# A float32 tanh-gated double matmul: the stores from the third triple on issued by ScalarE instead of SyncE

## The chip, the cores and the metric

The kernel runs on one core of a Trainium2 chip. A time is the device time of one execution in microseconds. Beside it there is one profiled execution, whose span (first to last instruction of the program) is a little shorter than its device time.

## The reference

```python
def reference(x, w1, w2):          # x (16, 512, 1024), w1 and w2 (1024, 768), all float32
    y1 = np.matmul(x, w1)
    y2 = np.matmul(x, w2)
    return (np.tanh(y1) * y2).astype(np.float32)
```

The 16 x 512 rows of `x` make 64 row tiles of 128. Each gives one output tile of 128 x 768 float32, 384 KB.

## The kernel before

**Arithmetic.** Inputs are cast to float16. The first four row tiles (`HEAD`) are multiplied plainly, eight matmuls for each block of columns. The other 60 go in 20 triples: the 3 row tiles of a triple, the two halves of the inner dimension and three blocks of 512 weight columns are combined by a scheme of the Strassen kind (`C_OPS`): 15 products of four matmuls each in place of 18. Its sums of x operands (`x_sum`, line 425) and of weights are made by VectorE, its sums of results (`c_add`, line 467) by VectorE and its signed copies between banks and SBUF (`c_copy`, line 461) by ScalarE. ScalarE also makes the tanh (`c_tanh`, line 470), VectorE multiplies it by the second result (`c_mul`, line 475), both into an output tile `o`. ScalarE further sums absolute values of every x tile and weight block (line 394), for a flag that would send odd inputs to a general path; it is not taken here.

**The data's way.** GpSimd loads a row tile from HBM with a cast (`load_x`, line 366) into one of 8 buffers `xh`; SyncE transposes it by DMA (`transpose`, line 391) into one of 12 buffers `xT`; GpSimd does not issue load `mt` before the transpose of tile `mt - 4` has landed (`hold_loads`, line 494). Output tiles lie in 9 buffers and go to HBM by `store` (line 431), one DMA for a tile; only those of the last triple and of one early tile go in parts.

**The order.** All instructions are written in an order made by `Planner`, a list scheduler in the kernel's Python. Each operation (`op`) gets its engines with a modelled cost, a due time, what it needs, and what it is to stand behind (`behind`, which sets the order alone). `PE_ORDER` fixes the order of the products. The program then issues each engine's instructions in that order. An engine's queue is in order: an instruction that waits holds up all behind it. The program's framework adds the waits: a store waits for the multiplies into its tile, a tanh for the landing of the store that had the same output buffer. It also gives the DMAs of SyncE and ScalarE eight semaphores in turn, and a DMA waits until the one that had its semaphore before, eight DMAs earlier in the program, has landed. DMAs of GpSimd have eight of their own.

**What the change touches.** Line 731 plans the store of every tile that is neither in the head nor in the last triple. There `i` is the triple, `late` a product of the next triple (`p0`, `p4` or `p12`) behind which the store is to stand. Lines 721, 723 and 729 plan the other stores, the split ones for SyncE or ScalarE as the planner finds room.

Of the kernel before, what the change touches and what calls it, by code (L numbers as in the profile page):

```python
# [74 lines left out]
class Planner:  # L75
# [9 lines left out]
    def op(self, name, engines, due, needs, fn, *args, behind=(), issued=(), chains=(), xfer=0.0, latency=None, seeds=False,  # L85
           lands=None, hold=0.0):
        assert name not in self.ops, name
        self.ops[name] = dict(engines=engines, due=due, needs=[n for n in needs if n], behind=[n for n in behind if n], issued=[n for n in issued if n], fn=fn, args=args,
                              chains=chains, xfer=xfer, latency=latency, seeds=seeds, lands=lands, hold=hold)
        for c in chains:  # L90
            self.chains.setdefault(c, {"left": 0, "bank": None, "end": 0.0, "act": 0.0, "dve": 0.0})["left"] += 1
# [154 lines left out]
def kernel(  # L246
# [66 lines left out]
    def xh_place(mt):  # L313
        return (mt - HEAD) % XH_BUFS
# [7 lines left out]
    op = plan.op  # L322
# [193 lines left out]
    slot_of = {(i, p): ORIGIN + z * SLOT for z, i, p in sequence}  # L516
# [4 lines left out]
    late = [f"b{k}" for s, k in slices if s == "b"]  # L521
# [8 lines left out]
    for n, what in enumerate(on_sp):  # L530
# [3 lines left out]
        else:  # L534
# [4 lines left out]
               behind=[f"c{a}{b}" for a, b in old], lands=lands[what])  # L539
# [3 lines left out]
    for n, mt in enumerate(rows_in):  # L543
        op(f"L{mt}", {"pool": 0.58}, 1 + 0.1 * n, [], load_x, mt, issued=[f"L{rows_in[n - 1]}" if n else f"c{late[-1]}"],
           behind=[f"cx{m}{h}" for m in range(2, HEAD) for h in range(2) if xh_place(m) == xh_place(mt)], lands=lands[f"x{mt}"])
# [8 lines left out]
    for t in range(2):  # L554
        for k in range(KO):
            late = START + 32 + 8 * (t * KO + k)
# [34 lines left out]
    outs = {mt: [] for mt in range(MT)}  # L591

    def reuse_out(mt):
        return [f"st{mt - O_BUFS}"] if mt >= HEAD + O_BUFS else []
# [16 lines left out]
    for n, s in enumerate("agb"):  # L611
        for mt in range(HEAD):
            if (s, mt) == ("b", HEAD - 1):
                continue
            due, behind = (lambda n: landed[slices["agb".index(s) * KO + n]] + 0.8 + 0.02 * mt), [FILL[mt]] if s == "b" and mt in FILL else []
            finals(mt, s, due(KO - 1) + (5.0, 3.0, 7.0)["agb".index(s)], plain(mt, s, due, behind))

    mt = HEAD - 1
# [57 lines left out]
    for i in range(TRIPLES):  # L676
# [3 lines left out]
        for v, a, b, how in A_SUMS:  # L680
            op(f"S{v}.{i}", {"dve": 0.335}, None, x_needs(i, a) + x_needs(i, b), x_sum, i, v, a, b, how,
               hold=needed(i, v) - S_AHEAD if i > 1 else 0.0,
               behind=[f"{r}.{i - S_BUFS}" for r in a_readers[v]] if i >= S_BUFS else first_done)
# [3 lines left out]
        for o in C_OPS:  # L687
# [19 lines left out]
            mt = HEAD + 3 * i + r  # L707
            due = soonest[i, name] + LAST
            if kind in ("t", "th"):
                lo, n = (0, F) if kind == "t" else (F, G)  # L710
                op(f"{name}.{i}", {"act": 0.5 if n == F else 0.285}, due, needs, c_tanh, i, r, o[4], lo, n, o[5],
                   behind=reuse_out(mt) + ([f"{FIRST_READER[name]}.{i}"] if i == TRIPLES - 1 and name in FIRST_READER else []), chains=chains)
# [4 lines left out]
    for mt in range(MT):  # L717
        i = (mt - HEAD) // 3 if mt >= HEAD else -1
        if mt < HEAD:
            kept = mt == HEAD - 1  # L720
            op(f"st{mt}", {"sp": 0.05}, 1e3, outs[mt][:1] if kept else outs[mt], store, mt, F if kept else 0, G if kept else N, behind=[f"p12.{4 + mt}"], xfer=1.0)
            for t in range(2 if kept else 0):
                op(f"st{mt}{chr(88 + t)}", {"sp": 0.4, "act": 0.4}, 2e4, outs[mt][1 + t:2 + t], store, mt, t * G, G, xfer=0.4)
            continue
        late = [f"{('p0', 'p4', 'p12')[(mt - HEAD) % 3]}.{i + 1}"] if i < TRIPLES - 2 else []
        if i == TRIPLES - 1:
            for a, lo, n in ((0, 0, F), (1, F, G)):
                part = outs[mt][a:a + 1]
                op(f"st{mt}{a}", {"sp": 0.4, "act": 0.4}, 2e4, part, store, mt, lo, n, xfer=0.4)
        else:  # L730
            op(f"st{mt}", {"sp": 0.05}, slot_of[max(i, 0), "p2"] + 12, outs[mt], store, mt, behind=late, xfer=1.0)
    for mt in range(BY_PE, MT):
        back = xh_before(mt)
        free = [] if back is None else ([f"PT{back}0", f"PT{back}1"] if back < BY_PE else [f"T{back}"]) + ([f"D{back}"] if back >= HEAD else [])
# [1 line left out]
        if mt >= BY_PE + FREE:  # L736
# [4 lines left out]
           behind=xt_readers[mt - XT_BUFS] if mt >= XT_BUFS and mt - XT_BUFS != HEAD - 1 else [], xfer=1.2, latency=1.0 if mt < HEAD + 6 else 3.0)  # L741
    for mt in range(HEAD, MT):
        i, r = divmod(mt - HEAD, 3)
# [126 lines left out]
```

## Time and profile before

| | us |
|---|---|
| median of 3 runs | 300.72 |
| lowest, highest run | 299.75, 303.65 |
| the profiled execution's own time | 299.0 |
| its span | 297.2 |

The profile names engines PE (TensorE; PEld its weight loads), DVE (VectorE), ACT (ScalarE), POOL (GpSimd) and SP (SyncE). A "q" behind a name (SPq, ACTq) is the engine's instruction queue: issuing a DMA or waiting for a semaphore is work of the queue and is not counted as busy. A DMA's issue has a duration of its own, and its landing (the moment its semaphore is complete) comes later. "A <- B: t, n, m" in the waits view says that A sat idle t us in n waits, the longest m, and that B ended them. In the table by stretch each row gives the stretch's length and then the busy time of each engine with the number of its instructions, the clock that TensorE was granted, the mean busy share of the DMA engines and the rate in GB/s. Matmul durations overlap, since matmuls are pipelined; the distance between their starts is the better measure.

The DMA part of the page:

| issue | queue | count | KB each | median us from issue to landing |
|---|---|---|---|---|
| stores | SP | 60 | 384 | 5.4 |
| loads of x with a cast | POOL | 60 | 256 | 6.7 |
| transposes | SP | 57 | - | 6.6 |
| last stores in parts | SP, ACT | 9 | 128 or 256 | 2.0 to 2.8 |

### The profile page before, as it was taken

To read this page: it belongs to the slowest core of one execution; us is meant where nothing else is said; L and a number is where in the kernel's file an instruction comes from. 1 tells how busy PE (TensorE), PEld (TensorE's weight loads), DVE (VectorE), ACT (ScalarE), POOL (GpSimd) and SP (SyncE) were. 2 spreads that over 40 slices of the span, in tenths; PEclk is the share of its full clock that TensorE was granted. 3 is DMA by queue.
4 is the path that set the end of the run, shared out by engine and by line. 5 is a ranking of instruction groups with operands and counts; after the bars stand their busy time and mean duration, and the time that the engine had idled before them with its cause. 6 is when DMAs were issued, how large, how long until landed. Compare 5 with 4: busy or idle time off the path is not lost. (4 is left out here: it accounts for less than half of the span.)

```text
span 297.2 us, 4671 instructions
## 1 busy us (share of the span) xinstructions
PE 289.5 (97%) x1385; PEld 133.4 (45%) x1385; DVE 254.9 (86%) x539; ACT 226.1 (76%) x454; POOL 51.7 (17%) x129
## 2 busy tenths in 40 slices
PE   7999999999999999999999999999999999999993
PEld 5444444444444444444444444444444444444442
DVE  1669999989999998979989899889889898988884
ACT  3577899699878879797797988768686776868451
POOL 0064036030112210303122121122020200000000
PEclk9999999999999999999999999999999999999999
DMA  6999999999999999999999999999999999741234
GB/s 230 387 298 198 173 158 216 192 166 197 193 238 217 252 228 270 270 171 306 183 220 199 226 292 218 283 278 251 165 279 113 271 85 270 229 161 52 108 140 164
DMA packets 84427, 63.51 MB, mean 214 GB/s; under 512 B 62768, under 2 KB 66608, under 8 KB 84400
## 3 DMA queue, kind: packets, MB, share of 16 engines
q1 hardware_dynamic: 73456, 44.71, 64.0%
q0 software_dynamic: 9792, 16.78, 38.0%
q10 hardware_dynamic: 1152, 1.70, 1.6%
q8 instruction: 11, 0.18, 0.3%
q14 instruction: 16, 0.13, 0.1%
HBM read 39.85 MB, written 25.17 MB: 219 GB/s over the span
## 5 line engine op out<-in xcount | busy, mean ns | idle before, releaser
L457 PE MATMUL bank<-b,early_x 128*128 128x512 f16 x640 | 148.3, 379 | 0.1
L457 PEld LDWEIGHTS <-early_x 128*128 128x128 f16 x800 | 78.2, 98 | 95.1 <-issue 0.7
L461 ACT ACTIVATE arena<-bank 128x512 f32<-128x512 f32 x100 | 59.1, 596 | 33.4 <-PE bank L457 33.3
L467 DVE TENSOR_TENSOR bank<-bank,arena 128x512 f32<-128x512 f32 x100 | 69.6, 696 | 15.5 <-ACT arena L461 7.3
L475 DVE TENSOR_TENSOR o<-o,bank 128x256 f32<-128x256 f32 (+1 forms) x120 | 63.2, 547 | 5.8 <-ACT o L470 5.5
L394 ACT ACTIVATE junk<-xh 128x1024 f16<-128x1024 f16 x60 | 63.3, 1055 | 0.1
L457 PEld LDWEIGHTS <-xT 128*128 128x128 f16 x400 | 39.0, 98 | 46.4
L457 PE MATMUL bank<-b,xT 128*128 128x512 f16 x240 | 58.3, 379 | 0.0
L494 POOL CAST held<-xT 128x1 f32<-128x1 f16 x54 | 15.1, 280 | 163.7 <-DMA xT<-xh 163.7
L470 ACT ACTIVATE o<-bank 128x256 f32<-128x256 f32 (+1 forms) x80 | 34.4, 437 | 12.0 <-DVE bank L467 7.1
L457 PE MATMUL bank<-wh,xT 128*128 128x512 f16 x160 | 41.1, 379 | 0.0
L457 PE MATMUL bank<-wh,early_x 128*128 128x512 f16 x160 | 40.9, 379 | 0.0
L366 POOL DMA_DIRECT2D xh<-in_x_dram x60 | 31.7, 528 | 16.0 <-issue 5.4
L425 DVE TENSOR_TENSOR early_x<-early_x,xT 128x512 f16<-128x512 f16 x80 | 33.5, 418 | 0.6
L461 ACT ACTIVATE bank<-bank 128x512 f32<-128x512 f32 x40 | 21.5, 575 | 7.2 <-DVE bank L467 6.6
L470 ACT ACTIVATE o<-arena 128x512 f32<-128x512 f32 x40 | 25.1, 627 | 1.0 <-DVE arena L467 1.0
L434 PE MATMUL bank<-wh,xT 128*128 128x512 f16 x72 | 18.4, 379 | 1.1 <-DVE wh L372 0.5
L425 DVE TENSOR_TENSOR early_x<-xT,early_x 128x512 f16<-128x512 f16 x40 | 16.7, 418 | 0.0
L425 DVE TENSOR_TENSOR early_x<-xT,xT 128x512 f16<-128x512 f16 x40 | 16.7, 417 | 0.0
L467 DVE TENSOR_TENSOR bank<-arena,bank 128x512 f32<-128x512 f32 x20 | 13.9, 695 | 3.2 <-ACT o L470 1.7
L467 DVE TENSOR_TENSOR arena<-bank,arena 128x512 f32<-128x512 f32 x20 | 13.7, 685 | 1.4 <-ACT arena L461 1.3
L467 DVE TENSOR_TENSOR arena<-arena,bank 128x512 f32<-128x512 f32 x20 | 13.6, 678 | 0.0
(49 smaller groups left out, 135.4 us busy)
## 6 DMA issues: line engine op xcount, KB each, us to landing
out_dram<-o SPq DMA_DIRECT2D x60, 384.0 KB, 5.4
xh<-in_x_dram POOLq DMA_DIRECT2D x60, 256.0 KB, 6.7
arena<-in_w_dram SPq DMA_DIRECT2D x12, 256.0 KB, 5.5
early_x<-in_x_dram SPq DMA_DIRECT2D x8, 256.0 KB, 5.0
arena<-in_w_dram ACTq DMA_DIRECT2D x4, 256.0 KB, 5.9
wh<-in_w_dram POOLq DMA_DIRECT2D x8, 128.0 KB, 5.7
xT<-xh SPq DMA_TRANSPOSE x57, 6.6
out_dram<-o SPq DMA_DIRECT2D x2, 256.0 KB, 2.8
```

The lines of the kernel that those rows point to most:

```text
L366: pin(nc.gpsimd.dma_start(xh(mt), xf[mt]))
L394: pin(nc.scalar.activation(junk[:, :src.shape[-1]], src, ACT.Abs, scale=scale, accum_out=sums[:, column:column + 1]))
L425: pin(engine[e].tensor_tensor(x_operand(i, v), x_operand(i, a), x_operand(i, b), OP[how]))
L434: pin(nc.tensor.matmul(bank(chain)[:, :rhs.shape[-1]], xt(mt)[:, k, :], rhs, start=first, stop=k == KO - 1, skip_group_check=True))
L457: pin(nc.tensor.matmul(place(i, dst), x_operand(i, a)[:, k, :], w_rhs(b, k), start=begins and k == 0, stop=k == KH - 1, skip_group_check=T ...
L461: pin(nc.scalar.activation(place(i, dst), place(i, src), ACT.Copy, scale=float(sign)))
L467: pin(nc.vector.tensor_tensor(place(i, dst), a, b, ALU.add if signs == (1, 1) else ALU.subtract))
L470: pin(nc.scalar.activation(out_tile(HEAD + 3 * i + r)[:, lo:lo + n], place(i, src)[:, :n], ACT.Tanh, scale=float(sign)))
L475: pin(nc.vector.tensor_tensor(o, o, place(i, src)[:, at:at + n], ALU.mult))
L494: pin(nc.gpsimd.tensor_copy(held, xt(mt)[:, 0, :1]))
```

## The change

One line of the plan: for triples 2 to 18 the store's engine is ScalarE, with a modelled cost of 0.35 us, instead of SyncE with 0.05.

```diff
         else:
-            op(f"st{mt}", {"sp": 0.05}, slot_of[max(i, 0), "p2"] + 12, outs[mt], store, mt, behind=late, xfer=1.0)
+            op(f"st{mt}", {"act": 0.35} if i >= 2 else {"sp": 0.05}, slot_of[max(i, 0), "p2"] + 12, outs[mt], store, mt, behind=late, xfer=1.0)
```

In the list of instructions, 51 stores leave SyncE's queue (147 instructions to 96) and stand in ScalarE's (389 to 440), each between two activations. The planner works with the new costs, so from the third triple on some neighbouring instructions of ScalarE and VectorE change places and products use other banks; the order of the products on TensorE stays. Which DMA is the eighth before another changes with the order too.

## The prediction

> **What bounds the kernel now.** I read the page first, its busy times and slices.
>
> ```profile
> span 297.2 us, 4671 instructions
> ...
> PE 289.5 (97%) x1385; PEld 133.4 (45%) x1385; DVE 254.9 (86%) x539; ACT 226.1 (76%) x454; POOL 51.7 (17%) x129
> ...
> PE   7999999999999999999999999999999999999993
> ...
> PEclk9999999999999999999999999999999999999999
> ```
>
> A busy TensorE alone proves little, so I looked at the starts of its matmuls one by one: 216 ns apart without a hole from 35.6 us to the last at 292.5 us, but for one gap of 0.1 us at 285.1. The waits view of PE for 36 to 292 us is empty. All the idle time of TensorE lies in the start (before 36 us, where nothing is edited: the first moved store stands near 74 us) and in the last 4.6 us. So no engine that works faster between 36 and 292 us can shorten the run. The change can only keep this row of matmuls closed or tear it.
>
> The table by stretch says how much room ScalarE has (its column is the fourth after the length).
>
> ```profile
> core 0: us, PE busy (x) PEld busy (x) DVE busy (x) ACT busy (x) POOL busy (x), PEclk, DMA share, GB/s
> ...
> 74.00:125.00 51.00, 51.00 (x238) 23.15 (x237) 46.47 (x98) 42.02 (x88) 9.69 (x26) 1.00 1.16 233
> 125.00:176.00 51.00, 51.00 (x238) 23.12 (x237) 44.75 (x94) 42.91 (x89) 9.76 (x24) 1.00 1.23 227
> 176.00:228.00 52.00, 52.00 (x243) 23.59 (x241) 46.29 (x97) 39.42 (x79) 9.40 (x26) 1.00 1.18 237
> 228.00:280.00 52.00, 52.00 (x244) 23.59 (x242) 46.60 (x101) 37.94 (x76) 2.85 (x8) 1.00 0.78 170
> ```
>
> A triple lasts 60 matmuls, 12.95 us. ScalarE is idle 9.0 of 51 us from 74 to 125 us, so 2.3 us in a triple, and 3.5 us in a triple at the end. It is the waits view that tells what this idleness is.
>
> ```profile
> ACT arena L461 <- PE bank L457: 28.8, 38, 2.9
> ACT bank L461 <- DVE bank L467: 5.5, 10, 0.6
> ```
>
> That is ScalarE of 74 to 280 us: it waits for matmuls (28.8 us), it is ahead. But not far: I followed, from the starts and ends in the timeline, how late each of its instructions could begin before a matmul would start late. The median is 1.0 us, the smallest outside the last triple 0.3 us. Example: the tanh of 102.77 us, then its multiply on VectorE 103.25 to 103.66, then the matmul into that bank at 103.99. A stall of ScalarE over one or two microseconds is a stall of TensorE.
>
> **The change part by part.** Removed: 51 issues from SyncE's queue (triples 2 to 18, three each). Added: the same 51, 384 KB each, on ScalarE's queue, in the instruction listing 3 between some 22 activations of a triple. The bytes are the same. Prices:
>
> ```profile
> L431 SPq DMA_DIRECT2D out_dram<-o x49: 362/529/1112, 75.0 to 255.5; - x49
> ...
> L391 SPq DMA_TRANSPOSE xT<-xh x45: 1232/2080/4261, 71.2 to 253.1; - x45
> ```
>
> These two are SyncE from 74 to 256 us (ns, least/median/most). *Issue on ScalarE:* its own final stores, smaller, took 338 to 363 ns, its loads at the start 406 to 460; the same 384 KB on SyncE 529. I take 0.53, the equal transfer; bounds 0.34 and 1.11. 3 x 0.53 = 1.6 us a triple against 2.3 us idle. It is no activation time, though: the records show ScalarE's queue taking its next instruction when the one before starts to run (a semaphore wait and an activation both at 96.42 us), so 0.53 us lies beside the 0.38 to 1.06 us of the activation ahead. Cost 0; with that cover gone, the idle 0.1 to 1.3 us before the next one and its slack still hide it.
>
> *Wait for the tile:* the planner puts a store behind a matmul of the following triple, so the multiplies it needs ended 0.7 to 7 us before (all but the last triples). Cost 0. In the last triple but one a store waits for its multiply (ended 277.5 us) ahead of a copy that ran at 277.74 with 0.25 us to spare: 277.5 + 0.34 to 0.53 is 0.15 us late to 0.04 us past the slack. Cost 0.
>
> *Wait for a semaphore:* this is what I think decides. In the listing the DMAs of SyncE and ScalarE share eight semaphores in turn, so each waits until the eighth before it has landed. On SyncE that held up nobody but transposes; on ScalarE it holds up the activations behind the store, then VectorE's multiplies, then TensorE's banks. I compared, by the times of before, when the eighth-last landed with when ScalarE gets there. Before 90 us it had landed 0.4 to 2 us earlier, after 180 us 2 to 27 us earlier, but from 94 to 175 us it lands up to 4.5 us later for 16 of 19 stores. The worst:
>
> ```profile
> 95.88 1.55 SPq L431 DMA_DIRECT2D out_dram<-o  x2
> ...
> 101.09 0.39 ACT L470 ACTIVATE o<-bank 128x256 f32<-128x256 f32 x1
> ```
>
> The second store of the first line (96.96 us, landed 105.59) is the eighth before a store that stands behind this tanh. 105.59 - 101.09 = 4.5 us late. The cover: the next activation ran at 102.77 and has 0.32 us of slack, less 0.53 of issue, 1.47 us. So 3.0 us of TensorE. The other fifteen lack less, up to 2.8 us. Upper bound if paid once: 3.0, since a TensorE that is 3.0 us later finds the next landings in time. Lower bound 0: that store stood on SyncE behind two moved ones (0.58 and 1.03 us of issue) and landed 8.6 us after issue against a median of 5.4; without them, 95.4 + 5.4 = 100.8 us, before ScalarE comes. I take the middle, **+1.5 us**, as the ends are equally near.
>
> *SyncE without the stores:* transposes wait 0.7 us on average from the landing of their rows to issue, and land 7.2 us after issue, partly behind stores. Both may shrink. TensorE doesn't feel it: transposed tiles of after 80 us land 2.8 us or more ahead of their first reader. Nothing gained. Should stores on a third queue slow the loads instead, that 2.8 us is the cover.
>
> *The end:* after the last matmul (292.5) come multiplies to 293.46, the last store (ScalarE already, issued 293.50, landed 296.15) and 1 us of closing. No edit there: 0, give or take 0.5.
>
> Sum: 299.0 (the profiled execution: span 297.2 and 1.8 around it) + 1.5 = 300.5. That execution was 1.7 us under the median of the runs shown, 300.72; on the median the forecast is **302.2 us**.
>
> **A page against the row.** At the start both queues issue at once:
>
> ```profile
> 0.75 1.81 SPq L351 DMA_DIRECT2D early_x<-in_x_dram  x4
> ...
> 0.75 1.86 ACTq L361 DMA_DIRECT2D arena<-in_w_dram  x4
> ```
>
> Eight issues in 1.86 us, each 0.39 to 0.46 us, where SyncE alone needed 0.33 to 0.43: beside plain loads a second issuer costs at most 0.1 us. None of before's rows has ScalarE issuing during a transpose. The Trainium skill (Perfetto Trace Analysis, "DMA Instruction — HWDGE (DVE, Sync)") says that one descriptor generator is shared by the issuing queues and locked for one instruction at a time; by that rule eight issues would have taken over 2.6 us, so for plain loads the row is against it, while for transposes it would make the second rival below.
>
> **The rivals.** *Waits that add up (slower).* If transposes are late again each time, because they too wait for TensorE to release their tile, the sixteen shortfalls are paid one by one: 20 us less the 2 of two stores whose eighth-last is itself moved, 18 us, so 320 on the median. For it: SyncE's transposes waited for matmuls at all (3.2 us, two times). Against: only two, and four tiles take 16.5 us through load and transpose while TensorE needs 17.3, so the landings gain on it. It decides once the transposes' pace is TensorE's.
>
> *A store behind a transpose's issue (slower).* A transpose holds SyncE 1.2 to 4.3 us, together about half the time from 74 to 253 us. If ScalarE's store must wait for the rest of it, then by the positions in before nine stores find 1.3 to 3.6 us left against 0.7 to 2.6 us of cover (worked out as above), an excess of 11 us in sum: 312 on the median. It decides where more than the cover is left; with transposes of 1.23 us, their length on an empty queue, hardly anything exceeds it and the time is the forecast's. For it: transposes do reach 4.3 us. Against: the start's row; and without stores ahead in their queue the transposes may go back to 1.23 us.
>
> *Faster.* Only the 4.6 us of the end and the start could give; over 2% is 6.0 us, so practically closed. A fraction of a microsecond from a luckier order at the end lies within the forecast.
>
> **How the numbers follow.** Forecast, waits absorbed once (+0 to +3.0): 0.64. Store behind a transpose: 0.21, from 302 to 312, mostly past 2% (306.7). Waits adding up: 0.12. Something that I don't see: 0.03, mostly faster. Two per cent is about what a measurement here can tell from no change. Faster 0.02; same 0.67 (the forecast and the mild end of the second rival); slower 0.31. The forecast's own range is 299.8 (nothing added, the lowest run shown) to 303.7 (+3.0 on the median). To hold 8 in 10, the range must take in most of the second rival: 299.5 to 311, with the adding rival outside.
>
> **What would show it.** Right: starts of matmuls still 216 ns apart but for a few holes, 0 to 3 us in sum, between 94 and 175 us, named ScalarE or VectorE; ScalarE's waits showing a landing ahead of a few stores there and none after 180 us; store issues on ScalarE of 0.35 to 0.6 us. The shared-issue rival: store issues on ScalarE of 1 us and more, each ending where a transpose ends. The adding rival: holes triple after triple. Wrong altogether: a closed row of matmuls with another length, or transposed tiles that come late.

## The result and the profile after

Before: 299.34 us, median of 6 runs (298.70 to 303.65). After: **313.9 us**, median of 6 runs (309.23 to 328.77). The ratio is 1.039, with a 95% interval of 1.036 to 1.043. The change makes the kernel slower. (Executions of one kernel differ, some being several per cent longer than the rest; every ratio here leaves the longer ones out, so a median can stand above its ratio.)

The profiled execution of after took 311.65 us, 12.65 more than that of before. The lines of its page that answer to those shown of before:

```profile
span 309.9 us, 4644 instructions
...
PE 294.8 (95%) x1385; PEld 134.7 (43%) x1385; DVE 255.0 (82%) x539; ACT 226.6 (73%) x454; POOL 51.3 (17%) x129
...
PE   8999999999949599999999999999999999999993
...
PEclk9999999999989969999999999999999999999999
```

ScalarE and VectorE are busy for as long as before (226.6 and 255.0 us; before 226.1 and 254.9), but the span is longer. One slice is worth 7.75 us; the 12th and the 14th of TensorE are half empty, and in or right behind each the clock dips. The stretches around these two places, in the table by stretch (columns as before: length, then busy time of each engine, clock, DMA share, GB/s):

```profile
core 0: us, PE busy (x) PEld busy (x) DVE busy (x) ACT busy (x) POOL busy (x), PEclk, DMA share, GB/s
...
74.00:125.00 51.00, 42.97 (x179) 18.21 (x177) 35.08 (x73) 31.65 (x67) 8.48 (x22) 0.90 1.22 215
125.00:176.00 51.00, 51.00 (x238) 23.12 (x237) 45.41 (x96) 42.91 (x88) 9.44 (x26) 1.00 1.14 234
85.40:90.00 4.60, 0.49 (x4) 0.10 (x2) 0.02 (x1) 0.65 (x2) 1.33 (x4) 1.00 1.14 225
90.00:93.60 3.60, 3.41 (x9) 1.16 (x9) 3.37 (x8) 3.35 (x6) 0.28 (x2) 0.53 1.12 245
104.50:108.60 4.10, 0.47 (x3) 0.10 (x1) 0.00 (x0) 0.56 (x2) 0.71 (x2) 0.84 1.30 205
108.60:114.00 5.40, 5.31 (x13) 1.79 (x13) 4.09 (x9) 3.97 (x9) 1.64 (x4) 0.50 1.07 280
```

From 74 to 125 us TensorE started 179 matmuls where before started 238; from 125 us on it is as full as before. In 85.4 to 90.0 nearly all engines stand still together, the DMA engines do not; then nine matmuls run at a granted clock of 0.53. The same again from 104.5 us. From the starts of the matmuls one by one: two steps of 4.49 us (from 85.50) and 4.10 us (from 104.59), 8.16 us more than two steps of 216 ns; and behind each, steps of 427 ns in place of 216 until 93.5 and 113.9 us, 4.8 us more. Together 13.0 us; the last matmul ends 12.6 us later than in before (305.19 against 292.56). So **two holes with what follows them are the whole loss**.

Who made them is in the waits view of after:

```profile
PE bank L457 <- ACT arena L461: 7.8, 2, 4.1
ACT arena L461 <- DMA xT<-xh: 7.0, 1, 7.0
ACT arena L461 <- DMA out_dram<-o: 6.5, 1, 6.5
```

TensorE waits twice for a copy of ScalarE (line 461), and that copy waits once 7.0 us for the landing of a transpose and once 6.5 us for the landing of a store. The copy reads and writes neither: it only stands behind a store in ScalarE's queue. ScalarE's timeline around the first (start, duration, engine, line, operation, in brackets the idle time before it and its releaser):

```profile
82.12 0.19 ACT L394 ACTIVATION_READ_ACCUMULATOR junk<-xh 128x1 f32 x1
88.95 0.35 ACTq L431 DMA_DIRECT2D out_dram<-o  x1
89.35 0.60 ACT L461 ACTIVATE arena<-bank 128x512 f32<-128x512 f32 x1 [7.03 <-DMA xT<-xh]
```

and around the second:

```profile
107.66 0.34 ACTq L431 DMA_DIRECT2D out_dram<-o  x1
108.05 0.60 ACT L461 ACTIVATE arena<-bank 128x512 f32<-128x512 f32 x1 [6.48 <-DMA out_dram<-o]
```

The first store is that of tile 10. It issues at 88.95 us, 0.02 us after the transpose of tile 21 has landed (issued 80.30, landed 88.93). The second is the store of tile 13; it follows the landing of the store of tile 0, which SyncE had issued at 99.76 and which landed at 107.58. In the order of the changed program these two DMAs are each the eighth before the waiting one.

### The profile page after: what moved, and what is told of

It reads as the page before. It is cut to its first block, busy times and chain, and to the rows that moved or that the text cites. A ratio compares the mean times of both kernels' runs of the same rounds, so it can differ in the third digit from the quotient of the medians.

```text
span 309.9 us, 4644 instructions
## 1 busy us (share of the span) xinstructions
PE 294.8 (95%) x1385; PEld 134.7 (43%) x1385; DVE 255.0 (82%) x539; ACT 226.6 (73%) x454; POOL 51.3 (17%) x129
## 5 line engine op out<-in xcount | busy, mean ns | idle before, releaser
L457 PE MATMUL bank<-b,early_x 128*128 128x512 f16 x640 | 150.0, 382 | 8.0 <-ACT arena L461 7.8
L457 PE MATMUL bank<-b,xT 128*128 128x512 f16 x240 | 59.4, 384 | 0.0
L457 PE MATMUL bank<-wh,early_x 128*128 128x512 f16 x160 | 42.6, 391 | 0.2 <-ACT bank L461 0.2
```

Source lines behind the costliest of these rows:

```text
L457: pin(nc.tensor.matmul(place(i, dst), x_operand(i, a)[:, k, :], w_rhs(b, k), start=begins and k == 0, stop=k == KH - 1, skip_group_check=T ...
```

## The experiments

Each ran on the same chip as runs of before taken with it, whose median was 298.9 to 299.2 us. "Hole" below is the excess over 216 ns of steps between matmul starts of over 1 us, "slow" that of shorter lengthened steps, mostly the 427 ns ones.

### Is it the new order of the operations, or the issue?

The change does two things: the planner gives neighbouring operations other places, and the stores are issued by ScalarE. One kernel does the first alone, the other the second alone.

```diff
 # plan only: the changed plan, the stores issued by SyncE
     def store(e, mt, lo=0, n=N):
+        e = "sp" if HEAD + 6 <= mt < MT - 3 else e
```

> Every engine's compute order is the changed kernel's, the planner books the stores on ScalarE, but SyncE issues them. Landing theory (a store on ScalarE waits for the landing of the eighth DMA before it and holds the activations behind it): no such wait can hold ScalarE, the matmuls are closed again, 298.5 to 301. Order theory (the reordered activations and multiplies cost the time): as the changed kernel, 309 to 313.

Measured: 299.68 us (298.95 to 311.41, 4 runs), ratio 1.000 (0.995 to 1.004). Its row of matmuls has no hole, only two steps, near 220 and 234 us, that are 0.6 and 0.7 us too long. The same stretch as above:

```profile
74.00:125.00 51.00, 51.00 (x238) 23.15 (x237) 46.52 (x98) 42.19 (x88) 9.75 (x25) 1.00 1.20 213
```

ScalarE runs its 348 activations here in just the order that it has in after. So the order costs nothing that shows.

```diff
 # issue only: the plan of before, the stores issued by ScalarE
     def store(e, mt, lo=0, n=N):
+        e = "act" if HEAD + 6 <= mt < MT - 3 else e
```

> The plan of before to the letter (the stores cost SyncE 0.05 us in it), and the same 51 stores issued by ScalarE at the places that this order gives. Landing theory: the store of tile 10 still stands eight DMAs behind the transpose of tile 21 and that of tile 13 behind the store of tile 0, so 308 to 314. Order theory: the order is that of before, so 299 to 301.

Measured: 315.13 us (311.80 to 324.15, 4 runs), ratio 1.041 (1.036 to 1.047): the whole loss. In its waits view (line 462 is line 461 of after):

```profile
ACT junk L394 <- DMA out_dram<-o: 19.4, 3, 14.0
PE bank L458 <- ACT arena L462: 15.3, 3, 11.1
ACT junk L394 <- DMA xT<-xh: 6.2, 1, 6.2
```

Now a sum of absolute values (line 394) is what stands behind the stores, and again it is let go by landings, once after 14.0 us. The holes of this execution (324.15 us) make 20.0 us, the slow steps 5.3; one hole of 2.3 us, at 78 us, is not of this kind, there TensorE itself waits for a transposed tile. What the waits hit depends on the plan, that they come does not.

### Which of the moved stores cost?

My sum had the shortfalls between 94 and 175 us, the theory of landings therefore expected the late stores to be free.

```diff
-{"act": 0.35} if i >= 2 else {"sp": 0.05}
+{"act": 0.35} if 2 <= i < 6 else {"sp": 0.05}   # early: 12 stores
+{"act": 0.35} if i >= 6 else {"sp": 0.05}       # late: 39 stores
```

> Only the 12 stores of triples 2 to 5 go to ScalarE. Landing theory: both long waits lie there, so the whole loss stays, 308 to 314. Issue theory: 12 of 51 parts, 302.

> Only the 39 stores of triples 6 to 18 go to ScalarE, the 12 of triples 2 to 5 stay on SyncE. Landing theory: the eighth DMA before is at most 2 to 3 us late there and ScalarE has about that much cover, so 298.5 to 301. Issue theory (each store costs ScalarE its issue): 39 of 51 parts of the 12.7 us, 308 to 310.

The early twelve: 313.54 us (307.15 to 319.46, 4 runs), ratio 1.028 (1.022 to 1.034). The profiled execution of 307.15 us has ScalarE standing 5.2 us ahead of the store of tile 10 (transpose of tile 21 again), 1.7 and 3.2 us ahead of two others; holes 5.0, slow 3.4. So the early stores alone bring most of the loss, as expected.

The late ones: 301.85 us once, and 318.56, 319.61 and 319.67 us; no ratio can be given. The expectation (298.5 to 301) was **missed**. The run of 301.85 us, just above the expectation, left no trace. The profiled execution (318.56) has waits of 6.0 us at 138, 4.6 at 159 and 6.2 us at 229 us. From its waits view:

```profile
ACT arena L461 <- DMA xT<-xh: 6.7, 2, 5.0
ACT junk L394 <- DMA xT<-xh: 6.6, 1, 6.6
ACT junk L394 <- DMA out_dram<-o: 6.4, 1, 6.4
```

The mechanism is the same, but the lead that landings had over ScalarE late in the execution of before is not there in this one: its median transpose took 7.8 us from issue to landing, against 6.6. One trace's landings are no property of the kernel.

To see whether there is a lead anywhere, the last 18 stores alone:

```diff
-{"act": 0.35} if i >= 2 else {"sp": 0.05}
+{"act": 0.35} if i >= 13 else {"sp": 0.05}
```

> Only the 18 stores of triples 13 to 18 go to ScalarE, where by the landings in before the eighth DMA has landed 2 to 20 us before ScalarE comes. Landing theory: the issue itself is hidden beside the activations, 298.5 to 300.5, unless a slow stretch of transfers outlasts that lead. Issue theory: 18 of 51 parts of the loss, 303 to 304.

Measured: 313.9 us (307.04 to 322.38, 4 runs), ratio 1.034 (1.026 to 1.041); **missed** again. In the profiled execution (316.93) there are waits of 7.5, 6.2 and 4.1 us at 226, 239 and 255 us, each ended by the landing of a transpose. This time something else was late as well:

```profile
ACT junk L394 <- DMA xT<-xh: 11.2, 2, 6.6
DVE early_x L425 <- DMA xT<-xh: 8.8, 2, 6.1
ACT o L470 <- DMA xT<-xh: 7.9, 1, 7.9
PE bank L457 <- DVE o L475: 6.8, 1, 6.8
```

VectorE itself waited 6.1 us for a transposed tile, until 223.3 us, in the same hole in which ScalarE stood ahead of its first moved store until 226.5; and a hole of 1.3 us at 207 us, also behind a late tile, precedes every moved store. From the issue of tile 44's transpose to that of tile 50's passed 31.4 us (175.3 to 206.7), against 20.9 in before, and up to there the program is still the same as before's. So the pace of the transfers differs between executions for a reason that I have not found, and only some of this kernel's 13.8 us of holes are the moved stores': the last 3 us of that one, and those behind the waits at 239 and 255 us.

### Is it the issue's own time, or the transfer behind it?

```diff
 # after; a moved store writes 128 of its 768 columns (the rest of the output is left out)
     def store(e, mt, lo=0, n=N):
+        n = P if HEAD + 6 <= mt < MT - 3 else n
```

> The changed kernel with its 51 stores all on ScalarE at the same places and with the same waits, but each writes 128 of its tile's 768 columns (the rest of the output is left out). Landing theory: with 16 MB less to move, transposes and stores land earlier than ScalarE comes to the store that waits for them; no long wait, 298.5 to 302. Issue theory (51 issues or the order cost the time): as the changed kernel, 308 or more.

Measured: 301.27 us (299.26 to 301.86, 5 runs), ratio 1.005 (1.001 to 1.009). All 51 issues are on ScalarE, at the same places; what is gone is five sixths of their bytes. The two waits of after are still there, for the same DMAs, but shortened from 6.6 and 6.1 us to 2.9 and 1.8; holes 2.1, slow 0.9, about the 2.8 us by which its span (300.0) is over that of before. The issues themselves therefore cost nothing that shows, and with fewer bytes on their way the waits for landings are shorter.

### Does a store on ScalarE overtake the transposes?

In after the transpose of tile 20, issued at 76.0, landed at 87.1 us, 11.1 us later; in before 6.4 us passed. A store of 384 KB that stood behind these transposes in SyncE's queue (tile 12, issued at 82.0 us) is now issued by ScalarE at 75.5, ahead of both. So put this one store back:

```diff
-{"act": 0.35} if i >= 2 else {"sp": 0.05}
+{"act": 0.35} if i >= 2 and mt != 12 else {"sp": 0.05}
```

> The changed kernel, but the first moved store, of tile 12, stays on SyncE, behind the transposes. If that store, issued 6 us earlier by ScalarE, is what made the transposes of tiles 20 and 21 land late: tile 21's lands near 85.8 us as before (not 88.9), the first long wait shrinks from 6.6 us by about 3 and the run by 3 to 5 us against the changed kernel. If not: both waits as in the changed kernel.

The place did what was expected: transpose of tile 20 in 6.6 us, of tile 21 landed at 83.8 us (after: 88.9), the wait ahead of tile 10's store 1.5 us (after: 6.6). The time decides nothing: 316.43 us (306.17 to 318.95, 4 runs; no ratio can be given), the shortest run 3 us under the shortest of after, the others longer than after's median. In the profiled execution (314.42) the next waits were longer instead:

```profile
ACT arena L461 <- DMA out_dram<-o: 8.2, 1, 8.2
ACT junk L394 <- DMA xT<-xh: 4.8, 1, 4.8
```

Over all kernels the transpose of tile 20 took 3.9 to 6.6 us where that store stands behind it on SyncE (before, plan only, the late stores and others). Where ScalarE issues it within 0.6 us ahead it took 11.1 us in after, 10.1 with the early stores, 15.6 with another turn (an experiment below) and 8.4 with the small stores. In issue only, the store went 5 us ahead and tile 20 took 6.8 us; there tile 21 took 9.0. Tile 21's transpose, for which the first long wait waits, landed at 87.6 to 89.3 us in after, early stores and issue only, and at 80.9 to 86.2 us where the store stayed on SyncE. That an overtaking store lengthens this wait is well supported; that every wait has such a cause is not.

### What does a hole cost TensorE?

My sum priced a hole at its own length. So before, with nothing moved, but a stall made by hand: extra activations on ScalarE ahead of one copy (`copy60.10` is its name in the plan).

```diff
     for n in order:
         if n not in soon:
+            if n == "copy60.10":
+                for _ in range(8):    # second kernel: 5
+                    pin(nc.scalar.activation(junk[:, :N], wh[:, 0, :N], ACT.Abs))
```

> The kernel before, with eight extra activations of 768 columns on ScalarE ahead of one copy of the eleventh triple: one stall of about 5.9 us (8 x 0.74), nothing else. Against 1.7 us of cover a hole of 4.2 us in the matmuls. If a hole costs only itself: 303.5. If TensorE runs at half its pace for some 3 us behind it: 305.5 to 306.

> The same with five extra activations: a stall of 3.7 us, a hole of 2.0 us. If the pace halves behind a hole of any such length: 303; if only behind longer ones: 301.

Eight: 308.34 us (306.34 and 310.33), ratio 1.031 (1.021 to 1.041). Five: 302.49 us (301.47 and 303.51), ratio 1.012 (1.006 to 1.018). The table by stretch of the first around its hole:

```profile
176.50:180.70 4.20, 0.15 (x1) 0.00 (x0) 0.00 (x0) 4.07 (x7) 1.43 (x4) 0.92 1.31 232
180.70:186.80 6.10, 6.02 (x14) 2.01 (x14) 4.23 (x10) 4.53 (x11) 0.71 (x2) 0.50 1.12 262
186.80:190.00 3.20, 3.20 (x16) 1.50 (x15) 2.80 (x7) 2.48 (x6) 0.90 (x3) 0.99 1.14 294
```

A hole of 4.29 us, and then 6.1 us at a clock of 0.50, in which 14 matmuls ran where 28 would have; 3.4 us more by the steps. The span is 7.4 over that of before. The traced execution, 306.34 us, is the one that half a pace behind the hole had been expected to give. With five there were two holes, 1.67 and 0.98 us, and half the clock followed as well:

```profile
178.00:179.00 1.00, 0.52 (x3) 0.28 (x3) 0.54 (x1) 0.95 (x2) 0.67 (x2) 1.00 1.11 413
...
181.00:182.00 1.00, 1.00 (x4) 0.31 (x3) 0.77 (x3) 1.00 (x2) 0.00 (x0) 0.50 1.28 287
```

Holes 2.6, slow 1.7; the two runs, 301.47 and 303.51 us, lie on either side of the two times expected. So a microsecond of hole cost 1.7 to 1.8 us here, where no DMA was moved, and 1.6 in after (13.0 for 8.16). In the other kernels with holes, holes and slow steps together are 1.3 to 1.7 times the holes, so this is no fixed price.

### Is it the turn of the semaphores?

If a store waits for a certain DMA because it has the same semaphore, another turn must let it wait for another DMA. Here the planner is told that loads and transposes land later, from the fifth triple on. The order of ScalarE's and VectorE's work stays as in after; SyncE's order and the turn change.

```diff
-op(f"L{mt}", ..., xfer=XX)
+op(f"L{mt}", ..., xfer=XX, latency=None if mt < HEAD + 13 else 6.0)
...
-   ..., xfer=1.2, latency=1.0 if mt < HEAD + 6 else 3.0)
+   ..., xfer=1.2, latency=1.0 if mt < HEAD + 6 else 3.0 if mt < HEAD + 13 else 6.0)
```

> The changed kernel with two modelled latencies of the plan changed (6 us each for the loads of x and the transposes from the fifth triple on). ScalarE's and VectorE's instructions and their order are exactly the changed kernel's; SyncE's transposes stand one or two places later against its own nine stores, and in the turn of the semaphores a younger transpose is now the eighth before: the store of tile 11 waits for the transpose of tile 22 (was: store of tile 8), that of tile 15 for 23, of tile 13 for 25, of tile 16 for 28, of tile 24 for 32. By the landings in before these are 6 to 8 us later than ScalarE comes. Landing theory: more and longer waits on ScalarE before 135 us than in the changed kernel, 318 to 335. If the eighth DMA is not what ScalarE waits for: as the changed kernel, 309 to 316.

Measured: 330.14 us (314.87 to 336.92, 4 runs; no ratio can be given). The times alone don't decide, since the shortest run lies in the rival's range (309 to 316); the trace does. ScalarE in the profiled execution (327.02 us):

```profile
83.25 0.19 ACT L394 ACTIVATION_READ_ACCUMULATOR junk<-xh 128x1 f32 x1
91.86 0.35 ACTq L431 DMA_DIRECT2D out_dram<-o  x1
92.26 0.60 ACT L461 ACTIVATE arena<-bank 128x512 f32<-128x512 f32 x1 [8.81 <-DMA xT<-xh]
```

In this kernel the eighth before the store of tile 10 is the transpose of tile 20, not 21. It landed at 91.84, the store issued at 91.86; tile 21 landed at 92.8 only. In after the same store issued 0.02 us after tile 21, and 1.8 us after tile 20. The store follows whichever DMA the turn names. Ten waits of 0.8 to 8.4 us, holes 19.6, slow 8.7.

The traces name the semaphore of every DMA, so this can be counted over all ten kernels in which ScalarE issues moved stores. ScalarE stood idle 0.8 us or more ahead of a moved store 53 times. Eight of these are one store, that of tile 60, which waits for its own tile. The other 45 times the store issued within 0.1 us after the landing of the DMA that had its semaphore before.

The other way, a mend: start loads earlier, so that transposes land earlier.

```diff
-    AHEAD, FREE = 4, 3
+    AHEAD, FREE = 6, 3
```

> The changed kernel, but GpSimd may issue a load once the transpose six tiles back has landed, not four: loads and transposes run further ahead of the products, the stores stay on ScalarE. Landing theory: the transposes of tiles 21 and 28 and the store of tile 0 land some 5 us earlier, both long waits go or shrink under the cover, 299 to 304. If the transfers only queue up longer, as many bytes being on their way: waits stay, 308 or more.

Measured: 371.52 us (361.43 to 385.42, 4 runs), ratio 1.214 (1.208 to 1.219). With six loads ahead in place of four they only queue up: from issue to landing the median transpose took 10.8 us (after 6.8), the median store 8.2 (after 5.3). From the waits view:

```profile
PE bank L457 <- ACT bank L461: 24.2, 6, 9.0
ACT bank L461 <- DMA xT<-xh: 21.2, 3, 8.4
PE bank L457 <- ACT arena L461: 17.3, 4, 10.7
ACT arena L461 <- DMA out_dram<-o: 13.3, 1, 13.3
```

Longer landings, longer waits of ScalarE; the holes make 48 us, of which 4.8 us, at 52 us, come ahead of every moved store: there VectorE waits 4.9 us for a transposed tile. The mend failed, and longer landings again went with longer holes.

### Stores on ScalarE without the wait

The last kernel keeps the stores on ScalarE and their bytes, and takes away what they wait for. The three output tiles of a triple lie side by side, and one DMA of 1152 KB stores them. That leaves 4 DMAs in a triple in place of 6, so the eighth before is the store of two triples earlier. The first triple whose stores are fused is the one where the kernel with the late stores began, which took 318.6 to 319.7 us in three of four runs and 301.85 in the other.

```diff
+    o_three = [once.tile([P, 3, N], f32, name=f"o{HEAD + 3 * j}") for j in range(O_BUFS // 3)]
+    o_bufs = [...the four of the head...] + [o[:, r] for o in o_three for r in range(3)]
...
+    def store_three(e, i):
+        a = HEAD + 3 * i
+        pin(engine[e].dma_start(of[a:a + 3].rearrange("t p n -> p t n"), o_three[i % (O_BUFS // 3)]))
...
-            op(f"st{mt}", {"act": 0.35} if i >= 2 else {"sp": 0.05}, ..., outs[mt], store, mt, behind=late, xfer=1.0)
+        elif i < 6:
+            op(f"st{mt}", {"sp": 0.05}, ..., outs[mt], store, mt, behind=late, xfer=1.0)
+        elif (mt - HEAD) % 3 == 2:
+            op(f"st{mt}", {"act": 0.35}, ..., outs[mt - 2] + outs[mt - 1] + outs[mt], store_three, i, behind=[p4 of the next triple], xfer=3.0)
```

> The output tiles of a triple lie side by side, and from the seventh triple on one DMA of 1152 KB on ScalarE stores all three, behind the product where the last of the three single stores stood; until then SyncE stores as in the kernel before. ScalarE still issues all of these stores, the bytes are the same, but a triple has 4 DMAs in the turn of the eight semaphores in place of 6: each store then waits for the store of two triples earlier, issued 26 us before (the first for the transpose of tile 33, which in the kernel before landed at 135.5 us, when the plan has the store at 135.4). It stands against the run with single stores on ScalarE from the same triple on (span 316.8 us, ScalarE waits of 6.0, 4.6 and 6.2 us ahead of stores). If the landing of the eighth DMA before is what tears the row: no wait of ScalarE for a landing over 0.5 us but perhaps for the first of these stores, the matmuls 216 ns apart, 298.5 to 301 us, whatever the pace of the transposes is as long as tiles come in time. If it is the stores' place on ScalarE itself, or their bytes overtaking loads and transposes: holes as in that run, or, since one store now brings three times as many bytes at once, longer ones; 305 us and more, with TensorE or VectorE waiting for xT.

Measured: 303.0 us (302.10 to 306.85, 4 runs), ratio 1.019 (1.009 to 1.028). ScalarE waited 0.8 us ahead of the first of these stores, for the transpose of tile 33 as worked out, and ahead of no other. That half of the expectation of landings held; the time, 298.5 to 301, did not quite. What is left is small and of the kind that the other theory named, waits for xT. The waits view from 130 to 290 us, three lines of it (line 462 is the product, 426 the sum of x operands):

```profile
PEld L462 <- DMA xT<-xh: 3.7, 3, 1.6
DVE early_x L426 <- DMA xT<-xh: 3.6, 4, 1.6
PE bank L462 <- DMA xT<-xh: 2.3, 3, 1.1
```

Three times TensorE waits for a transposed tile itself. The lengthened steps between matmuls are 0.52, 0.93, 0.99 and 1.48 us, the first where ScalarE had waited 0.8 us; 3.05 us over four steps of 216 ns, about the 2.9 us by which the last matmul is later than in before (295.50 against 292.56). The median transpose took 8.1 us to land (before 6.6):

```profile
out_dram<-o ACTq DMA_DIRECT2D x13, 1152.0 KB, 8.5
out_dram<-o SPq DMA_DIRECT2D x21, 384.0 KB, 5.5
...
xT<-xh SPq DMA_TRANSPOSE x57, 8.1
```

So in these two traces the effects stand apart. With the wait in ScalarE's queue, the late stores tore holes of 12.6 us, with 7.3 us of slow steps (span 316.8); with all but 0.8 us of it gone, late tiles were left, and 3.1 us of span (300.3). The times by themselves don't show it: the one run of 301.85 us of the late stores is as short as the shortest of this kernel, and no trace tells how long ScalarE waited in it. The fused stores are no gain over before either: a row of matmuls that was closed from 36 to 292 us could not become shorter, and none of these kernels beats it.

## Why the prediction was wrong, by its steps

**The bound.** Right. TensorE's row could only be torn, and its tears and their slow aftermath are the whole 12.6 us.

**ScalarE's room.** Right: a stall of one or two microseconds of ScalarE is one of TensorE's. The two long waits, 7.0 and 6.5 us of idle time, became holes of 4.27 and 3.89 us.

**The issue, 0.53 us, cost 0.** The cost was right (small stores). The duration was high: the view of line 431 in after gives least/median/most in ns as

```profile
L431 ACTq DMA_DIRECT2D out_dram<-o x55: 338/338/542, 75.5 to 306.1; - x55
```

**The wait for the tile, cost 0.** Right, and the place was the one named: ahead of tile 60's store, in the last triple but one, ScalarE stood 2.67 us until VectorE's multiply ended at 290.13 us, and the store issued at 290.16. The waits view gives this wait to TensorE, as the copy behind the store needed a matmul too. No step between matmuls there is lengthened.

**The wait for a semaphore, +1.5, at most 3.0.** This is the step that failed. The mechanism was the right one, the term measured 13.0 us: 8.16 of holes and 4.8 of slow steps. Four things in it were wrong.

- *The turn.* I had named tile 0's store as the eighth before the store that stands behind the tanh of 101.09 us, 4.5 us late. In the list of the changed program that store is tile 18's, and the eighth before it is the store of tile 11; what follows tile 0's store in the turn is the store of tile 13, 6 us earlier. With ScalarE's order of after and a closed row (plan only), ScalarE is free for it at 95.55; tile 0's store landed at 105.59 in before. That is a shortfall of 10 us, which the list and before's landings would have shown. Likewise the store of tile 10 waits for the transpose of tile 21: landed 85.7 in before, ScalarE free at 82.4 in plan only, 3.3 us late at a place that I had counted as safe ("before 90 us it had landed 0.4 to 2 us earlier").
- *"Paid once".* The two waits are for different DMAs, and the second was 6.1 us though TensorE was by then 6 us late: tile 0's store, on SyncE behind two transposes whose issues took from 93.62 to 99.71, issued only at 99.76 and landed 7.8 us later. My lower bound had it land at 100.8, freed of the two stores ahead of it.
- *Landings taken from before.* The stores on ScalarE overtake transposes and change what they wait for (tile 20: 6.4 us to 11.1).
- *The price of a hole.* I put down its length; in after it was 1.6 times that, as the half clock follows. No row of before could show it, since before had no hole.

**SyncE without the stores.** I expected its transposes no slower; their median went from 6.6 to 6.8 us, and the two behind tile 12's store, those of tiles 20 and 21, took 11.1 and 8.6 us in place of 6.4 and 5.7. In after no product waited for a transposed tile (VectorE once, 0.2 us), so the cover of 2.8 us held; with the fused stores it didn't.

**The end.** Right: 4.7 us from the last matmul to the end of the span, as in before.

**The store behind a transpose's issue.** Wrong as a rival, and the row on which I doubted the rule was the better guide. The timeline of after shows both at once:

```profile
93.62 2.90 SPq L391 DMA_TRANSPOSE xT<-xh  x1
...
93.88 0.34 ACTq L431 DMA_DIRECT2D out_dram<-o  x1
```

The store is issued in 0.34 us, 0.26 us after the start of a transpose's issue that goes on to 96.52. Sixteen of the moved stores begin inside such an issue and take 338 to 352 ns. Nor did the transposes' issues go back to 1.23 us: their median is 1.75 us, 1.73 in before. The lock of which the Trainium skill speaks (Perfetto Trace Analysis, "DMA Instruction — HWDGE (DVE, Sync)") isn't seen between these two; here the measurement decides.

**The waits that add up.** The rival with the right sign and mechanism, at 0.12. Its form was not that of after (two waits, not one in each triple), but the waits are indeed paid one by one, and in three other kernels (issue only, the other turn, six loads ahead) four to ten of them are. Its ground against, "the landings gain on it", was read from one execution.

**The numbers.** 302.2 us forecast, 299.5 to 311 as range; 313.9 measured, above it. What the trace of before could have told me stands in its view of the line of the stores

```profile
DMA to landing us min/median/max: 2.0/4.8/12.6
```

and in that of the line of the transposes:

```profile
DMA to landing us min/median/max: 3.1/6.6/14.4
```

Landings that spread over ten microseconds, 51 new waits for them, and a queue with a float of 1.0 us in front of the bound: the end of the range belonged far above 311.

**Still open** is why transfers are slower in one execution than in another, as in the run of the last 18 stores against before up to 207 us, where the programs are the same. Whether that alone is why the late stores took 302 us once and 319 us otherwise is not shown.

## What to carry to other kernels

Before a DMA is moved to a computing engine's queue, write out from the changed program's own list what it waits for there, the reuse of its semaphore included, and compare the spread of that landing (not one landing) with the float of what stands behind it in the queue; an issue of 0.34 us was free, the wait in front of it was not. On an engine that computes, a DMA should wait only for what landed long ago: fewer and larger DMAs put the one before it in the turn far enough back. And a hole in a dense row of matmuls can cost more than its length, here 1.3 to 1.8 times.

## What the runs showed of the hardware

After the two holes of after and those of both stalled kernels, TensorE's matmuls of 512 columns start 427 ns apart in place of 216, at a granted clock of 0.50, for 3 to 6 us: 3.5 and 5.2 us in after, 6.1 and 3.0 us with the stalls made by hand. Not every hole is followed by it, and its length alone doesn't decide. With five extra activations it followed two holes of 1.67 and 0.98 us, and in the kernel that keeps tile 12's store on SyncE one of 2.20 us at 122 us. A hole of 3.11 us at 102 us in the kernel with another turn and one of 2.26 us at 78 us in issue only were followed by a granted clock of 1.00, and so were the holes of 0.3 to 1.3 us of the fused stores. The Trainium skill (TensorE: Matmul & The Clock Gate, "What's actually happening") has the clock go down after an idle window of about 3.4 us in a free-running count. In the kernel with five extra activations TensorE's longest idle time at that place was 1.50 us, and the clock was halved all the same; so there it took less than a whole window without work, and the runs don't show what the condition is.

A store that ScalarE issues is not held up in its issue by a transpose's issue on SyncE (338 to 352 ns). It can lengthen the transposes' landing instead, by 4 to 5 us for tile 20 in after and with the early stores. It shares the transfers with them: tile 12's store took 8.0 us to land in after and 5.6 in before. And with six loads ahead in place of four the median transpose took 10.8 us to land in place of 6.8.
